# Half of the output gate's projection moves into the row-by-row stage of q, k and v, and group sums continue in PSUM

## The chip, the cores and the metric

The kernel runs on one core of a Trainium2 chip. The metric is the device time of one execution in microseconds; of several runs the median is taken. The engines are PE (matrix products), DVE (VectorE), ACT (ScalarE), POOL (GpSimd) and SP, whose queue issues the transfers here. PSUM is the memory in which PE adds up its products; SBUF is the memory that all engines share.

## The reference

The reference is a trunk of two layers in float32, with 256 rows (`S`) and 2048 columns (`DM`). Layer 0 has an mLSTM mixer and a squared-ReLU MLP, layer 1 a gated recurrence and an MLP. Each of the four sublayers norms its input and modulates it by a scale, a shift and a gate that are products of `silu(c)` with a 2048 x 6144 matrix (`ada`). What matters here is the mixer of layer 0:

```
def mlstm_mixer(h, w_in, b_gate, norm_g, w_out):
    proj = h @ w_in
    q, k, v, o, ig, fg = jnp.split(proj, [1024, 2048, 4096, 6144, 6152], axis=-1)   # 8 heads
    ...
    hh = mlstm_chunkwise(q, k, v, li, lf)          # two chunks of 128 rows, state carried over
    hh = hh * lax.rsqrt(jnp.mean(hh * hh, axis=-1, keepdims=True) + EPS)
    hh = hh.reshape(B, S, V_W) * norm_g
    return (hh * jax.nn.sigmoid(o)) @ w_out
```

(The split points are written out as numbers, and the reshaping is left out.) `o`, the output gate, is a product of `h` with 2048 columns of `w_in`; it is needed only where the heads are done. `ig` and `fg` feed the recurrence of the stabilised weights (`li`, `lf`).

## The kernel before

The product of every weight matrix runs over tiles of 128 x 2048 floats (1 MB). A tile comes by one transfer into a buffer (`raw`, four buffers, in `weights()`, L146), ACT rounds each half of it to a shorter format (`whi`, L153), and DVE forms the rest (`wlo`, L154). Activations are split in the same way (`pair`, L163 and L164). Three products, `whi` with both parts of the pair and `wlo` with the upper one, then replace one full product (`mm3`, L172 to L174). A tile may also go to PE unsplit, as one full float32 product (`direct`, the tile `wdir`): PE takes longer for it, ACT and DVE do nothing.

The modulation vectors are 192 more tiles of 1 MB (`adaraw`), which share the four buffers. Each is multiplied and summed by one DVE instruction (L113). They are needed step by step through the whole program and are spread over it as filler: `fill()` after a tile of weights issues the next adas at a rate, and `need()` issues those that the next step cannot do without. The rate comes from `QKV_RATE` in the first stage and later from `PACE`, which says how many adas are to be done at the end of each stage (56 at the end of stage `o`, 66 in `out0`).

The SP queue issues the transfers in the order of the program's lines. On the other engines a scheduler fixes the order of the instructions beforehand, by its own model of costs; the weights' split and the adas have a raised priority there. At run time every engine works its list from front to back, and an instruction that waits holds up all behind it.

The stages that the change touches:

- **Groups.** The normed input `h` comes as 16 chunks of 128 columns, and each needs its own two adas first. So q, k and v are computed by rows of the weight matrix: `GROUPS` = (2, 4, 4, 4, 2) chunks at a time (`group()`), each group with all 4096 columns of q, k, v. A group of n chunks takes 2n tiles (4, 8, 8, 8, 4; 32 in all); eight of these are direct (`DIRECT`, tile numbers). A group's sum for some columns is formed in PSUM, and `put()` takes it over: in the first group ACT copies it to SBUF (L390), in the later ones DVE adds it to what lies there (L392; 128x256 for q and k, 128x512 for v).
- **The gate block and its rows.** After the fourth group comes the block `wg` (L178 and L179) with the columns of `ig` and `fg`, then row arithmetic on eight partitions in DVE, then `rows` goes to DRAM (`rows_d`) and one column of it comes back to all partitions (`mlast`). From that and from the transposes of `g` (`gp`, L513, copied to `gT`) comes `wk` (L517, L518). The last group's products stand behind the gate block and are interleaved with this by the scheduler.
- **The heads.** Eight heads follow, each in parts: `scores`, `state` (`kw` and `cp`, L535 and L553), `head`, `meansq`, and after each second head `normed`, `gated`, which multiplies with the gate and forms the pairs `zs`. Between these parts stand the output gate's 16 blocks (`wo`, `ogate()`); the table `OB` says how many come at each of the 17 places. Each block ends in a tanh on ACT.
- **The output product.** 16 blocks of `awo` on the 16 z pairs, with the residual (L303) and the next norm; then the MLP.

Of the kernel before, what the change touches and what calls it, by code (L numbers as in the profile page):

```python
# [8 lines left out]
F32 = mybir.dt.float32  # L9
# [6 lines left out]
P = 128  # L16
# [24 lines left out]
GROUPS = (2, 4, 4, 4, 2)  # L41
DIRECT = (0, 1, 2, 3, 5, 8, 11, 14)

OB = (1, 1, 1, 1, 0, 1, 1, 1, 0, 1, 1, 1, 0, 1, 1, 1, 0)

QKV_RATE = (2, 1, 1, 0.75, 0)
PACE = dict(o=56, out0=66, w1a=82, w1b=90, mlp0=160, mix1=174, out1=176, mlp1=192)
# [3 lines left out]
def trunk_kernel(ctx, tc, xT_d, par_d, ada_d, wqkv_d, wg_d, wo_d, awo_d, bwi_d, bg_d, bwo_d,  # L51
# [335 lines left out]

    def put(dst, src, first):
        if first:
            A.activation(dst, src, AF.Copy)  # L390
        else:
            V.tensor_tensor(out=dst, in0=src, in1=dst, op=ALU.add)  # L392

# [8 lines left out]
    def group(gi, h32):  # L402
        gn, k0, nt = GROUPS[gi], sum(GROUPS[:gi]), 2 * sum(GROUPS[:gi])
        width = DM // gn
        for nb in range(2 * gn):
            direct = nt in DIRECT
            gh = h32 if direct else [[p[:, 0, :], p[:, 1, :]] for p in hs[k0:k0 + gn]]
            if direct:
                w = wpool.tile([P, DM], F32, name="wdir", tag="raw")
                nc.sync.dma_start(out=w, in_=wqkv_d[nt])  # L410
            else:
                w = weights(wqkv_d[nt])
            nt += 1

            def part(kk, o, n):
                if direct:
                    return [w[:, kk * width + o:kk * width + o + n]]
                o += kk % (gn // 2) * width
                return [t[:, o:o + n] for t in w[kk * 2 // gn]]

            def product(out, pairs, kk):
                ops = [(l, m) for a, l in enumerate(pairs[0]) for b, m in enumerate(pairs[1]) if a + b < 2]
                for n, (l, m) in enumerate(ops):
                    PE.matmul(out, lhsT=l, rhs=m, start=kk + n == 0,  # L424
                              stop=kk == gn - 1 and n == len(ops) - 1)

            for c0 in range(0, width, min(width, 512)):
                col = nb * width + c0
                if col < 2 * H * DQK:
                    for jj in range(min(width, 512) // P):  # L430
                        acc = ps.tile([P, S], F32, name="mm")
                        for kk in range(gn):
                            product(acc, (part(kk, c0 + jj * P, P), gh[kk]), kk)
                        n = col // P + jj
                        put(qk[n // 2][:, n % 2, :], acc, gi == 0)
                else:
                    n = min(width, 512)
                    for t in range(2):
                        acc = ps.tile([P, n], F32, name="mm")
                        for kk in range(gn):  # L440
                            product(acc, ([a[:, t * P:(t + 1) * P] for a in gh[kk]],
                                          part(kk, c0, n)), kk)
                        dst = vs[(col - 2048) // 512 * 2 + t].rearrange("p a b -> p (a b)")
                        o = (col - 2048) % 512
                        put(dst[:, o:o + n], acc, gi == 0)
            fill(1, QKV_RATE[gi])
# [8 lines left out]
    with ExitStack() as mctx:  # L455
# [130 lines left out]

        ths, hbs, zs = [], [], []
        obs = [0]

        def ogate(n):  # L590

            for _ in range(n):
                j = obs[0]
                obs[0] += 1
                acc = block([wo_d[j]], hs, mm3)
                if j % 2 == 0:
# [20 lines left out]

        pace("o", 16)
        ogate(OB[0])
# [220 lines left out]
```

## Time and profile before

| | |
|---|---|
| median of 3 runs | 2254.61 us (2252.55 to 2256.29) |
| profiled execution, its own time | 2257.06 us |
| its span | 2255.4 us |
| mean granted clock of PE | 0.991 |
| PE, DVE, ACT busy | 97%, 77%, 53% of the span |
| first matmul of group 1 | 61.51 us |
| end of the gate block | 214.1 us |
| `wk` | 254.53 us |
| last z pair | 380.1 us |
| end of the output product | 471.6 us |

All stages that the change touches lie in the first 472 us. Positions are counted from the start of the span. Busy time of PE is modelled: a matmul's record includes the drain of its pipeline, so records overlap. DVE's records, too, are a little longer than the spacing at which the same instructions follow each other. Windows of the profile give, for a stretch of time, the busy time of each engine with the number of its instructions, the clock granted to PE (1 is full speed), the busy share of the transfer engines, and what they moved in GB/s. In the chain of waits each row is a start, a duration and the work that held up the end; in groups of instructions, a row ends with the idle time just before the group's instructions and what ended it.

### The profile page before, as it was taken

What the parts mean: (1) busy time and instruction counts of PE and PEld (TensorE: products, weight loads), DVE (VectorE), ACT (ScalarE), POOL (GpSimd) and SP (SyncE); (2) the same over time, 40 slices, a digit from 0 to 9 for tenths busy, and PEclk for the clock granted to TensorE, in tenths of its full rate; (3) what the DMA queues carried; (4) which work ended last, traced back from release to release, by engine and by line L of the source; (5) the groups of instructions that cost most, each with busy time, mean ns of one, the idle gap of its engine ahead of it and who ended that gap; (6) DMA issues with size and microseconds to landing.
All of it is one profiled execution on the core that took longest, in us unless ns stands there. A gap on an engine that the chain in (4) does not pass through costs nothing.

```text
span 2255.4 us, 33736 instructions
## 1 busy us (share of the span) xinstructions
PE 2190.8 (97%) x13402; PEld 1942.1 (86%) x13402; DVE 1740.0 (77%) x2290; ACT 1194.7 (53%) x1845; POOL 79.4 (4%) x70
## 2 busy tenths in 40 slices
PE   7999999999999999999999999999999999999997
PEld 5788899898888888888888889888888888888886
DVE  5899899888998778888889898879775555555554
ACT  4334575454763336664445677756664334665443
POOL 0000000200000000000010000110000000000110
PEclk9999999999999999999999999999999999999999
DMA  9997788889788889888897677657776555555552
GB/s 341 340 345 286 276 308 327 322 291 329 272 303 317 317 317 329 324 322 320 310 323 251 225 241 267 222 205 260 281 280 205 187 187 188 188 189 191 188 188 101
DMA packets 85598, 601.24 MB, mean 267 GB/s; under 512 B 10424, under 2 KB 10552, under 8 KB 13120
## 3 DMA queue, kind: packets, MB, share of 16 engines
q1 hardware_dynamic: 84864, 598.03, 73.9%
q8 instruction: 105, 1.72, 0.3%
q10 hardware_dynamic: 576, 1.05, 0.1%
q14 instruction: 53, 0.43, 0.1%
HBM read 596.93 MB, written 2.11 MB: 266 GB/s over the span
## 4 chain that ended last, share of the span: by engine, by line
PE 81%; DVE 8%; DMA 5%; ACT 3%; issue 3%; POOLq 0%; DVEq 0%; SPq 0%; ACTq 0%
PE mm L178 40%; PE mm L179 21%; PE mm L424 6%; PE mm L174 3%; DVE wlo L154 3%; PE mm L173 3%; PE mm L172 3%; DMA adaraw<-in_ada 3%; DVE adaraw L113 2%; ACT whi L153 1%; PE mm L196 1%; PE mm L195 1%; PE mm L197 1%; DVE hmod L278 0%; DVE pair L167 0%
## 5 line engine op out<-in xcount | busy, mean ns | idle before, releaser
L178 PE MATMUL mm<-pair,whi 128*128 128x512 f32 x4352 | 1528.9, 395 | 7.1 <-DVE pair L167 5.5
L179 PE MATMUL mm<-pair,wlo 128*128 128x256 f32 x4352 | 1218.9, 281 | 9.2 <-DVE wlo L154 9.1
L154 DVE TENSOR_TENSOR wlo<-raw,whi 128x1024 fp32r<-128x1024 f32 x722 | 876.9, 1223 | 355.7 <-ACT whi L153 354.3
L153 ACT ACTIVATE whi<-raw 128x1024 fp32r<-128x1024 f32 x722 | 760.3, 1058 | 707.4 <-PE mm L178 503.1
L178 PEld LDWEIGHTS mm<-pair,whi 128*128 128x128 f32 x4352 | 817.1, 188 | 199.3 <-DVE pair L167 4.5
L179 PEld LDWEIGHTS mm<-pair,wlo 128*128 128x128 f32 x4352 | 819.1, 188 | 15.6 <-DVE wlo L154 13.6
L113 DVE SCALAR_TENSOR_TENSOR adaraw<-adaraw,cbc 128x2050 f32<-128x2050 f32 x192 | 439.6, 2290 | 74.4 <-DMA adaraw<-in_ada 63.4
L174 PE MATMUL mm<-pair,wlo 128*128 128x256 f32 x880 | 250.4, 285 | 3.0 <-DVE wlo L154 3.0
L172 PE MATMUL mm<-pair,whi 128*128 128x256 f32 x880 | 250.9, 285 | 2.4 <-ACT whi L153 2.4
L173 PE MATMUL mm<-pair,whi 128*128 128x256 f32 x880 | 250.6, 285 | 0.0
L174 PEld LDWEIGHTS mm<-pair,wlo 128*128 128x128 f32 x880 | 168.9, 192 | 3.7 <-DVE wlo L154 3.6
L172 PEld LDWEIGHTS mm<-pair,whi 128*128 128x128 f32 x880 | 168.7, 192 | 3.4 <-ACT whi L153 2.6
L173 PEld LDWEIGHTS mm<-pair,whi 128*128 128x128 f32 x880 | 168.9, 192 | 0.1
L303 DVE SCALAR_TENSOR_TENSOR xall<-mm,mod,xall 128x256 f32<-128x256 f32 x171 | 82.1, 481 | 36.5 <-PE mm L179 25.7
L312 ACT ACTIVATE hsum<-hsum 128x256 f32<-128x256 f32 x124 | 50.6, 414 | 107.9 <-DVE hsum L229 95.9
L258 POOL TENSOR_TENSOR nacc<-nacc,nsq 128x256 f32<-128x256 f32 x52 | 64.1, 1233 | 379.9 <-ACT nsq L249 369.8
L424 PE MATMUL mm<-pair,whi 128*128 128x256 f32 x384 | 69.5, 287 | 4.7 <-ACT whi L153 3.7
L424 PEld LDWEIGHTS mm<-pair,whi 128*128 128x128 f32 x384 | 59.0, 192 | 6.7 <-ACT whi L153 5.0
L424 PE MATMUL mm<-whi,pair 128*128 128x512 f32 x192 | 62.0, 399 | 0.6 <-DVE qk L392 0.6
L256 POOL TENSOR_TENSOR nacc<-nsq 128x256 f32<-128x256 f32 x4 | 6.3, 1568 | 1451.2 <-ACT nsq L249 1451.2
L164 DVE TENSOR_TENSOR pair<-hsum,pair 128x256 fp32r<-128x256 f32 x128 | 52.8, 419 | 1.9 <-ACT pair L163 1.5
L163 ACT ACTIVATE pair<-hsum 128x256 fp32r<-128x256 f32 x128 | 52.5, 415 | 3.2
(197 smaller groups left out, 1521.6 us busy)
## 6 DMA issues: line engine op xcount, KB each, us to landing
raw<-in_w SPq DMA_DIRECT2D x220, 1024.0 KB, 5.2
adaraw<-in_ada SPq DMA_DIRECT2D x192, 1025.0 KB, 7.0
raw<-in_w1a SPq DMA_DIRECT2D x32, 1024.0 KB, 7.0
raw<-in_bwi SPq DMA_DIRECT2D x28, 1024.0 KB, 5.1
raw<-in_wqkv SPq DMA_DIRECT2D x24, 1024.0 KB, 7.1
raw<-in_wo SPq DMA_DIRECT2D x16, 1024.0 KB, 7.0
raw<-in_awo SPq DMA_DIRECT2D x16, 1024.0 KB, 7.2
raw<-in_bwo SPq DMA_DIRECT2D x16, 1024.0 KB, 4.9
```

The costliest lines, as they stand in the source:

```text
L113: V.scalar_tensor_tensor(out=raw, in0=raw, scalar=1.0, in1=cbc, op0=ALU.mult, op1=ALU.mult, accum_out=mod[i][:, j:j + 1])
L153: A.activation(hi, sl, AF.Copy)
L154: V.tensor_tensor(out=lo, in0=sl, in1=hi.bitcast(F32), op=ALU.subtract)
L164: V.tensor_tensor(out=lo, in0=src, in1=hi.bitcast(F32), op=ALU.subtract)
L172: PE.matmul(out, lhsT=whi, rhs=p[:, 0, :], start=first, stop=False)
L173: PE.matmul(out, lhsT=whi, rhs=p[:, 1, :], start=False, stop=False)
L174: PE.matmul(out, lhsT=wlo, rhs=p[:, 0, :], start=False, stop=last)
L178: PE.matmul(out, lhsT=whi, rhs=p.rearrange("p a t -> p (a t)"), start=first, stop=False)
L179: PE.matmul(out[:, 0:S], lhsT=wlo, rhs=p[:, 0, :], start=False, stop=last)
L258: G.tensor_tensor(out=self.acc, in0=self.acc, in1=sq, op=ALU.add)
L303: V.scalar_tensor_tensor(out=xT[j], in0=acc[:, a:a + S], scalar=mod[i][:, 32 + j:33 + j], in1=xT[j], op0=ALU.mult, op1=ALU.add)
L424: PE.matmul(out, lhsT=l, rhs=m, start=kk + n == 0, stop=kk == gn - 1 and n == len(ops) - 1)
```

## The change

The first stage now also computes 1024 of the output gate's 2048 columns (`OG` = 8 blocks of 128). A group of n chunks takes 2.5 n tiles (5, 10, 10, 10, 5; 40 in all), and the number of tiles per group is `per`. Direct are now the five tiles of group 0 alone; the other 35 are split. The eight `wo` blocks left stand one to a head, after `state`. The four SBUF tiles of the moved half (`ob`) get their tanh in place, 128x512 each.

`put()` is gone. A sum is now 128x512 throughout: two column blocks of 256 side by side for q, k and the gate, 512 columns for v. From group 1 on, ACT first copies the sum so far from SBUF into PSUM, PE goes on adding to it (`start` is false for all its products), and ACT copies the result back. That makes 80 copies into PSUM and 100 out of it; the 96 additions on DVE are gone.

The rates `QKV_RATE` become (1.6, 0.8, 0.8, 0.4, 0) per tile, so 8, 8, 8 and 4 adas are issued with groups 0 to 3 (before 8, 8, 8 and 6); with four that group 0 needs in advance 32 adas lie before the heads, before 34. `PACE` is as it was: 56 are done after the heads. So 24 adas (before 22) are spread over 8 blocks of `wo` (before 16).

```diff
-DIRECT = (0, 1, 2, 3, 5, 8, 11, 14)
+DIRECT = (0, 1, 2, 3, 4)
+OG = 8
-OB = (1, 1, 1, 1, 0, 1, 1, 1, 0, 1, 1, 1, 0, 1, 1, 1, 0)
+OB = (0, 1, 0, 1, 0, 1, 0, 1, 0, 1, 0, 1, 0, 1, 0, 1, 0)
-QKV_RATE = (2, 1, 1, 0.75, 0)
+QKV_RATE = (1.6, 0.8, 0.8, 0.4, 0)
...
-    def put(dst, src, first):
-        if first:
-            A.activation(dst, src, AF.Copy)
-        else:
-            V.tensor_tensor(out=dst, in0=src, in1=dst, op=ALU.add)
+    ob = [act.tile([P, 2, S], F32, name="th", tag="act") for s in range(OG // 2)]
...
-        gn, k0, nt = GROUPS[gi], sum(GROUPS[:gi]), 2 * sum(GROUPS[:gi])
+        gn, k0 = GROUPS[gi], sum(GROUPS[:gi])
+        per = (4096 + OG * P) // 512
+        nt = per * k0 // 4
         width = DM // gn
-        for nb in range(2 * gn):
+        for nb in range(per * gn // 4):
...
-                    PE.matmul(out, lhsT=l, rhs=m, start=kk + n == 0,
-                              stop=kk == gn - 1 and n == len(ops) - 1)
+                    PE.matmul(out, lhsT=l, rhs=m, start=clear and kk + n == 0,
+                              stop=kk == gn - 1 and n == len(ops) - 1, skip_group_check=True)
...
+                for t in range(2):
+                    acc = ps.tile([P, 512], F32, name="mm")
+                    if col < 2048:
+                        dst = qk[col // 256 + t]
+                    elif col < 4096:
+                        dst = vs[(col - 2048) // 512 * 2 + t]
+                    else:
+                        dst = ob[(col - 4096) // 256 + t]
+                    dst = dst.rearrange("p a b -> p (a b)")
+                    if gi > 0:
+                        A.activation(acc, dst, AF.Copy)
+                    if 2048 <= col < 4096:
                         for kk in range(gn):
                             product(acc, ([a[:, t * P:(t + 1) * P] for a in gh[kk]],
-                                          part(kk, c0, n)), kk)
+                                          part(kk, c0, 512)), kk, gi == 0)
+                    else:
+                        for jj in range(2):
+                            for kk in range(gn):
+                                product(acc[:, jj * S:(jj + 1) * S],
+                                        (part(kk, c0 + (2 * t + jj) * P, P), gh[kk]), kk,
+                                        gi == 0 and jj == 0)
+                    A.activation(dst, acc, AF.Copy)
             fill(1, QKV_RATE[gi])
...
-        obs = [0]
+        obs = [OG]
+        ths = list(ob)
+        for th in ths:
+            A.activation(th, th, AF.Tanh, scale=0.5)
...
-        pace("o", 16)
+        pace("o", 16 - OG)
```

The line numbers of the new file are some six to ten higher from the groups on, and one higher before.

Three places show how the order of the engines' lists moves. The first is SP's list in the stage of the heads, where `in_wo` is a block of the output gate, `in_ada` an ada, and `MB` the rows that a head needs. Before:

```order
70 L526 DMA MB<-rows_d 128x512
71 L146 DMA raw<-in_wo 128x2048
72 L111 DMA adaraw<-in_ada 128x2050
73 L526 DMA MB<-rows_d 128x512
74 L146 DMA raw<-in_wo 128x2048
75 L111 DMA adaraw<-in_ada 128x2050 x2
76 L146 DMA raw<-in_wo 128x2048
77 L111 DMA adaraw<-in_ada 128x2050
78 L526 DMA MB<-rows_d 128x512
```

After:

```order
63 L532 DMA MB<-rows_d 128x512
64 L147 DMA raw<-in_wo 128x2048
65 L112 DMA adaraw<-in_ada 128x2050 x3
66 L532 DMA MB<-rows_d 128x512
67 L147 DMA raw<-in_wo 128x2048
68 L112 DMA adaraw<-in_ada 128x2050 x3
69 L532 DMA MB<-rows_d 128x512
```

A head had about two blocks and three adas between its `MB` and the next; it now has one block and three adas.

The second is DVE's list around `wk` and the first heads (`E`, `qw`, `em` and `rs` belong to a head). Before:

```order
208 L113 SCALAR_TENSOR_TENSOR adaraw,mod_127<-adaraw,cbc 128x2050
209 L154 TENSOR_TENSOR wlo<-raw,whi 128x1024 x2
210 L517 TENSOR_TENSOR wk<-gT,mlast 128x8
211 L113 SCALAR_TENSOR_TENSOR adaraw,mod_127<-adaraw,cbc 128x2050
212 L542 SCALAR_TENSOR_TENSOR E<-sp,E 128x256
213 L545 SCALAR_TENSOR_TENSOR qw<-qk_187,qw 128x128
214 L113 SCALAR_TENSOR_TENSOR adaraw,mod_127<-adaraw,cbc 128x2050
```

After:

```order
123 L114 SCALAR_TENSOR_TENSOR adaraw,mod_127<-adaraw,cbc 128x2050
124 L155 TENSOR_TENSOR wlo<-raw,whi 128x1024
125 L523 TENSOR_TENSOR wk<-gT,mlast 128x8
126 L155 TENSOR_TENSOR wlo<-raw,whi 128x1024
127 L114 SCALAR_TENSOR_TENSOR adaraw,mod_127<-adaraw,cbc 128x2050 x2
128 L155 TENSOR_TENSOR wlo<-raw,whi 128x1024
129 L551 SCALAR_TENSOR_TENSOR qw<-qk_187,qw 128x128
130 L548 SCALAR_TENSOR_TENSOR E<-sp,E 128x256
131 L155 TENSOR_TENSOR wlo<-raw,whi 128x1024 x2
132 L551 SCALAR_TENSOR_TENSOR qw<-qk_187,qw 128x128
133 L114 SCALAR_TENSOR_TENSOR adaraw,mod_127<-adaraw,cbc 128x2050
```

The weight halves of the last group now stand on both sides of `wk`, and two adas follow it ahead of the first head's own work.

On PE, `gp` (the transposes of `g`, which `rows` and `wk` follow) moves at the same place. Before, it stood ahead of the last three of group 4's 144 products (96 of 256 columns, 48 of 512):

```order
575 L424 MATMUL mm<-whi,pair 128x512 x2
576 L424 MATMUL mm<-wlo,pair 128x512
577 L424 MATMUL mm<-whi,pair 128x512
578 L513 MATMUL gp<-ident,g 128x8 x2
579 L424 MATMUL mm<-whi,pair 128x512
580 L424 MATMUL mm<-wlo,pair 128x512
```

After, it stands behind 96 narrow and 20 wide products of 192 (144 narrow, 48 wide):

```order
844 L425 MATMUL mm<-whi,pair 128x512 x2
845 L425 MATMUL mm<-wlo,pair 128x512
846 L519 MATMUL gp<-ident,g 128x8
847 L425 MATMUL mm<-whi,pair 128x512
848 L519 MATMUL gp<-ident,g 128x8
849 L425 MATMUL mm<-whi,pair 128x512
850 L425 MATMUL mm<-wlo,pair 128x512
```

The rest of group 4's v and all of its gate columns follow `gp`.

The third is ACT's list at the same place, in the kernel after (L440 is the copy into PSUM, L451 the copy out of it, L597 the tanh of the moved half):

```order
269 L440 ACTIVATE mm<-th 128x512
270 L154 ACTIVATE whi<-raw 128x1024 x2
271 L451 ACTIVATE v_202<-mm 128x512
272 L524 ACTIVATE wk<-wk 128x8
273 L440 ACTIVATE mm<-th 128x512 x2
274 L451 ACTIVATE th<-mm 128x512
275 L541 ACTIVATE kw<-kp,wk 128x128
276 L451 ACTIVATE th<-mm 128x512
277 L597 ACTIVATE th<-th 128x512 x2
```

ACT's part of `wk` stands ahead of the last two copies into PSUM; before, no product of the groups waited for ACT beyond the weights' upper halves.

More of the change, by code (lines that the diff above doesn't have):

```diff
@@ L419, in part, with product @@
                 return [t[:, o:o + n] for t in w[kk * 2 // gn]]
-            def product(out, pairs, kk):
+            def product(out, pairs, kk, clear):
                 ops = [(l, m) for a, l in enumerate(pairs[0]) for b, m in enumerate(pairs[1]) if a + b < 2]
                 for n, (l, m) in enumerate(ops):
-                    PE.matmul(out, lhsT=l, rhs=m, start=kk + n == 0,
-                              stop=kk == gn - 1 and n == len(ops) - 1)
-            for c0 in range(0, width, min(width, 512)):
+                    PE.matmul(out, lhsT=l, rhs=m, start=clear and kk + n == 0,
+                              stop=kk == gn - 1 and n == len(ops) - 1, skip_group_check=True)
@@ L428, in group @@
+            for c0 in range(0, width, 512):
                 col = nb * width + c0
[L429 to L439, printed above, removed]
+                for t in range(2):
[10 more added lines that the diff above has]
+                    if 2048 <= col < 4096:
@@ L440, in group @@
                         for kk in range(gn):
                             product(acc, ([a[:, t * P:(t + 1) * P] for a in gh[kk]],
-                                          part(kk, c0, n)), kk)
-                        dst = vs[(col - 2048) // 512 * 2 + t].rearrange("p a b -> p (a b)")
-                        o = (col - 2048) % 512
-                        put(dst[:, o:o + n], acc, gi == 0)
+                                          part(kk, c0, 512)), kk, gi == 0)
[5 more added lines that the diff above has]
+                                        gi == 0 and jj == 0)
@@ L585, in meansq @@
             V.scalar_tensor_tensor(out=out, in0=ss, scalar=1.0 / DV, in1=em, op0=ALU.mult, op1=ALU.add)
-        ths, hbs, zs = [], [], []
-        obs = [0]
+        hbs, zs = [], []
+        obs = [OG]
+        ths = list(ob)
+        for th in ths:
+            A.activation(th, th, AF.Tanh, scale=0.5)
         def ogate(n):
@@ L594, in ogate @@
                 obs[0] += 1
-                acc = block([wo_d[j]], hs, mm3)
+                acc = block([wo_d[j - OG]], hs, mm3)
                 if j % 2 == 0:
@@ L803 @@
     for gn in GROUPS:
-        w = w_in[k0 * P:(k0 + gn) * P, 0:4096].reshape(gn, P, 2 * gn, DM // gn)
-        qkv.append(w.transpose(2, 1, 0, 3).reshape(2 * gn, P, DM))
+        cs = 4096 + OG * P
+        w = w_in[k0 * P:(k0 + gn) * P, 0:cs].reshape(gn, P, cs * gn // DM, DM // gn)
+        qkv.append(w.transpose(2, 1, 0, 3).reshape(cs * gn // DM, P, DM))
         k0 += gn
@@ L814 @@
         "wg": cols(wg)[0],
-        "wo": cols(w_in[:, 4096:6144]),
+        "wo": cols(w_in[:, 4096 + OG * P:6144]),
         "awo": cols(a["a_w_out"][0]),
```

## The prediction

> **What bounds the kernel now.** I read the stages first (busy time of each engine in stretches that I cut at group 1's first matmul, at the ends of the groups, at `wk`, at the last z pair and at the split of the ninth `awo` tile), then the chain of waits inside them, then the groups of instructions by line.
>
> ```profile
> core 0: us, PE busy (x) PEld busy (x) DVE busy (x) ACT busy (x) POOL busy (x), PEclk, DMA share, GB/s
> 0.00:61.50 61.50, 44.11 (x160) 31.19 (x160) 33.08 (x45) 26.96 (x59) 0.70 (x6) 0.94 0.90 340
> 61.50:112.20 50.70, 50.68 (x257) 39.73 (x257) 43.76 (x60) 15.15 (x22) 0.00 (x0) 0.97 0.90 340
> 112.20:163.40 51.20, 49.02 (x282) 41.81 (x280) 48.03 (x64) 18.71 (x24) 0.00 (x0) 1.00 0.94 353
> 163.40:214.10 50.70, 49.88 (x314) 44.98 (x315) 47.89 (x60) 20.16 (x23) 0.00 (x0) 1.00 0.87 321
> 214.10:254.50 40.40, 36.48 (x249) 32.36 (x248) 35.28 (x64) 15.98 (x19) 0.00 (x0) 1.00 0.52 176
> 254.50:380.10 125.60, 124.38 (x985) 120.99 (x986) 118.95 (x167) 83.68 (x158) 8.28 (x8) 0.99 0.89 327
> 380.10:426.10 46.00, 40.60 (x313) 39.99 (x312) 43.02 (x69) 20.33 (x35) 10.61 (x6) 0.93 0.89 318
> 426.10:471.70 45.60, 45.60 (x388) 45.57 (x387) 36.76 (x38) 21.52 (x27) 10.48 (x8) 1.00 0.90 322
> ```
>
> Up to 61.5 transfers set the pace (340 GB/s, PE idle for 17.4 of 61.5 us). In the rows of groups 1 to 3 (61.5 to 214.1) PE is busy for all but 3.0 us, with DVE close behind (48 of 51); ACT has more than half free. In 254.5 to 380.1, the heads with the output gate's blocks between them, PE and DVE are both nearly full: 124.4 and 119.0 of 125.6. From 426 on PE alone is the bound. So the program has one stage in which neither PE nor DVE has room, and the change takes PE work out of that stage but leaves most of its DVE work.
>
> ```profile
> L113 DVE SCALAR_TENSOR_TENSOR adaraw<-adaraw,cbc 128x2050 f32<-128x2050 f32 x22 | 50.2, 2284 | 0.0
> L113 DVE DVE_READ_ACCUMULATOR adaraw<-adaraw,cbc 128x1 f32 x22 | 1.8, 80 | 0.0
> L154 DVE TENSOR_TENSOR wlo<-raw,whi 128x1024 fp32r<-128x1024 f32 x30 | 36.1, 1223 | 0.7 <-ACT whi L153 0.7
> L113 DVE SCALAR_TENSOR_TENSOR adaraw<-adaraw,cbc 128x2050 f32<-128x2050 f32 x7 | 16.0, 2285 | 0.0
> L154 DVE TENSOR_TENSOR wlo<-raw,whi 128x1024 fp32r<-128x1024 f32 x14 | 17.2, 1258 | 1.0 <-ACT whi L153 1.0
> ```
>
> The first three rows are DVE's groups of 254.5 to 380.1, the last two those of 380.1 to 426.1. Adas and weight halves are 88 of its 119 us in the first of these stages; the other 30.9 are the attention's own.
>
> **Group 0 (start of group 1).** The change puts 5 whole tiles ahead of group 1 where there were 4, with the same 8 adas (1.6 times 5, before 2 times 4). A tile of 1.05 MB at 340 GB/s takes 3.1 us, so group 1 starts 3 to 5 us later; I take 65.5 in place of 61.5. The fifth tile's products (some 6.8 us) lie in PE's idle time there.
>
> **Groups 1 to 3 and the gate block.** Split tiles replace four direct ones, and six more tiles come in.
>
> ```profile
> 69.01 7.07 PE L424 MATMUL mm<-hdirect,wdir 128*128 128x256 f32 x32
> 213.80 0.28 PE L179 MATMUL mm<-pair,wlo 128*128 128x256 f32 x1
> 61.51 1.27 PE L424 MATMUL mm<-pair,whi 128*128 128x256 f32 x5 [3.72 <-ACT whi L153]
> 61.50:65.10 3.60, 3.59 (x16) 3.31 (x17) 3.08 (x5) 2.03 (x4) 0.00 (x0) 0.53 0.96 392
> ```
>
> The stretch 163.4 to 214.1 holds eight split tiles and the gate block (its last matmul is the second row): 50.7/9 = 5.63 us for a tile. A direct one is the first row, about 6.8 us without the drain of its last matmul. Before, groups 1 to 3 and the gate block are 20 x 5.63 + 4 x 6.8 + 5.63 = 145 us and took 152.6, so 7 us were lost: about 2 at the start, where the clock was 0.53 for 3.6 us after 3.72 us of idle PE (last two rows), the rest to late halves on DVE. After: 31 x 5.63 = 174.5. Of the losses I keep 4, since DVE's additions go:
>
> ```profile
> L392 DVE TENSOR_TENSOR qk<-mm,qk 128x256 f32<-128x256 f32 x48 | 18.7, 418 | 2.9 <-PE mm L424 2.5
> L392 DVE TENSOR_TENSOR v<-mm,v 128x512 f32<-128x512 f32 x24 | 16.0, 684 | 2.4 <-PE mm L424 2.3
> L153 ACT ACTIVATE whi<-raw 128x1024 fp32r<-128x1024 f32 x44 | 45.4, 1056 | 51.5 <-PE mm L424 28.1 <-DMA raw<-in_wqkv 17.1 <-PE mm L178 3.4
> L390 ACT ACTIVATE v<-mm 128x512 f32<-128x512 f32 x8 | 4.8, 597 | 11.0 <-PE mm L424 11.0
> ```
>
> These additions are 34.7 us of DVE in 152.6, standing between its weight halves. In their place ACT copies each sum into PSUM and out again. Out of PSUM a 128x512 copy took 0.597 us (last row). Into PSUM none is in the trace: below by the 128x256 addition's 0.418, above by the 128x1024 copy's 1.056 us; nearest in shape and engine is the 0.597 row, which I take. (The Trainium skill, "ScalarE: Activation LUTs", says that ScalarE writes PSUM faster than SBUF; no row of this trace shows a write to PSUM of this size. By it the copy would be under 0.6.) ACT then has for a tile of four chunks 2 x 1.06 + 4 x 0.60 + 0.3 (its share of `hdirect` and pairs) = 4.8 us against PE's 5.63: covered, and in the order the copies in stand one or two units ahead of PE. Transfers: 10 tiles and 8 adas at 3.1 us are 55.8 against 56.3 of PE, so the cover is thin and half of the 4 us kept is for that. The gate block then ends at 65.5 + 178.5 = 244, before at 214.1.
>
> **From the gate block to wk.** Here the path is rows arithmetic, two small transfers, and `wk`.
>
> ```profile
> 239.20 0.29 PE L513 MATMUL gp<-ident,g 8*128 8x8 f32 x2
> 242.28 4.66 DMA rows_d<-rows
> 246.95 7.55 DMA mlast<-rows_d
> 254.53 0.18 DVE wk L517
> L517 DVE TENSOR_TENSOR wk<-gT,mlast 128x8 f32<-128x8 f32 x1 | 0.2, 169 | 2.9 <-DMA mlast<-rows_d 2.9
> ```
>
> Before it takes 40.4 us: 25 to `gp` (behind all but three of group 4's products on PE), 3 to the rows' transfer, 12.2 to `wk`. After, the order puts `gp` behind 116 of 192 products of group 4, 96 narrow and 20 wide: 2 tiles and 20/24 of one, 16 us at 5.63. But group 4 (two chunks) does four units per tile, so ACT needs 2.1 + 8 x 0.6 = 6.9 us where PE needs 5.6; I take 17 (16 to 20). DVE's side, some 10 us of rows arithmetic and four halves, fits in that. So `wk` comes at 244 + 17 + 3 + 12.2 = 276, 21.7 us later than the 254.5 of before, while eight of sixteen `wo` blocks, 45 us of PE, are already done. The wait for `mlast` now has more behind it: ACT's `wk` stands ahead of the last copies into PSUM, so PE's last units of group 4 wait too.
>
> **The heads.** From `wk` on DVE is the longer of the two. By the order it runs, from `wk` to the split of the ninth `awo` tile, 30 adas and 36 halves; before it was 29 and 44 (the five rows above). That is the core of it: eight blocks less take away eight halves in this stretch (the others' halves lay before `wk` or are replaced by the `awo` tiles' own), and the adas, three per block now, are as many as ever.
>
> ```profile
> 132.87 2.22 DVE adaraw L113 x2
> 222.19 2.28 DVE wlo L154 x2
> 164.22 44.23 PE mm L424 x280
> ```
>
> At the spacing of the chain (2.22 for an ada with its accumulator, 1.14 for a half) and with 30.9 + 9.2 us of other work (busy time of the two stages without these groups), DVE's work in this stretch was 29 x 2.22 + 44 x 1.14 + 40.1 = 154.6 of the 171.6 us that it took, with 17.0 of gaps; now it is 30 x 2.22 + 36 x 1.14 + 40.1 = 147.7. PE per head needs 5.63 + 4.6 = 10.2 us (4.6 from 124.4 less 15.5 tiles, over eight heads), DVE 3 x 2.22 + 2 x 1.14 + 3.9 = 12.8, transfers four tiles and 0.25 MB, 13.0. So PE idles some 2.7 us in each head, transfers are level with DVE, and the gaps that DVE had from a full PE shrink while some from transfers come. I take gaps of 10, with 0 and 17 as ends.
>
> **Sum.** The ninth `awo` tile is split at 276 + 147.7 + 10 = 434 in place of 426.1: 7.6 us later. From there on PE is the bound and the program is the same (56 adas at the end of the heads, then the same pace), so nothing is won back. The four tanh of 128x512 replace eight of 256 and cost ACT nothing that shows. The profiled execution took 2257.06 us (span 2255.4) and would become 2264.7; it lies 2.4 above the median of 2254.61, to which I add the 7.6: **2262 us**.
>
> The Trainium skill ("Perfetto Trace Analysis", Optimization Strategy) says that where the most contended engine changes between regimes, interleaving the regimes may help. By it this change goes the wrong way for the heads: it takes PE's work out from between DVE's. The stage rows agree as far as they go.
>
> **Rivals.** *A, PE is the bound throughout and DVE's relief is a gain.* For it: PE is busy for 97% of the whole span,
>
> ```profile
> PE 2190.8 (97%) x13402; PEld 1942.1 (86%) x13402; DVE 1740.0 (77%) x2290; ACT 1194.7 (53%) x1845; POOL 79.4 (4%) x70
> ```
>
> and DVE loses 34.7 us of additions in groups 1 to 3 alone. Then the idle PE of the six stages 61.5 to 426.1 goes (0.0 + 2.2 + 0.8 + 3.9 + 1.2 + 5.4 = 13.5), four direct tiles become split (4 x 1.2 = 4.7), and group 0 does 6.8 us of work in 4: together 21, 2234 us; with half of it, 2244. Against it: adas and attention's DVE work stay after `wk`. The Trainium skill ("Perfetto Trace Analysis", Optimizing Scalar/DVE Operations) has the rule that work moves to ScalarE where DVE is saturated; DVE's rows agree before 214 only. *B, a wash.* If ACT doesn't hold group 4 (16 in place of 17), groups 1 to 3 lose 2 less, and gaps are 7, the sum is 276 - 3 + 147.7 + 7 - 426.1 = 1.6: 2256 us. *C, ACT becomes the bound, and the time is longer still.* If the copy into PSUM costs 1.06, a four-chunk tile needs 2.1 + 1.2 + 2.1 + 0.3 = 5.7 (level with PE) and one of group 4 2.1 + 2.4 + 4.2 = 8.7 against 5.6: 2.8 tiles to `gp` cost 9 us more than PE's own, 8 more than I allow; with the 7.6, 2270. It decides from 0.75 us for that copy on. The same 2269 comes if the gaps stay at 17. *D, PE's clock.* Idle of 2.7 us in each head may bring what the 0.53 row shows, at 1.7 us a time; PE's slack of 2.7 covers it, so I give it nothing of its own.
>
> **How the numbers follow.** About 0.2%, 4.5 us, is what a measurement of this kernel can tell from no change. The forecast (4.5 to 12 us more) has 0.36, C and equal gaps (over 12) 0.15, B (within 4.5) 0.27, A in whole or part 0.22. Faster 0.22, same 0.27, slower 0.51. The likeliest case alone is 2259 to 2267; the range reaches down to half of A and up past C: 2243 to 2274.
>
> **What would show it.** Right: group 1's first matmul at 64 to 67; gate block's end at 241 to 247; `wk` at 272 to 281; between `wk` and the last z pair DVE busy for over 90% and PE for under 85%; the ninth `awo` tile's split 3 to 12 us later than before; the rest shifted as a whole. The additions' place in groups 1 to 3 shows ACT at 75 to 85%. Wrong: PE busy for over 95% in the heads (A); ACT busy for over 95% in groups 1 to 4 (C); the later part of the program not shifted but shorter or longer by itself, or `wk` before 268.

## The result, and the profile after

The changed kernel took 2276.19 us (median of 4 runs, 2271.14 to 2277.94) beside 2253.58 us for the kernel before on the same chip: a ratio of 1.0096 with a 95% interval of 1.0069 to 1.0123. It is slower by 1.0%, some 22 us. The forecast was slower by 7.6 us, and the measured time lies above the range. The profiled executions are 2275.65 us (span 2273.9) and 2257.06 us (span 2255.4).

The stages of the changed kernel, cut at the same events as those of before (the second to fourth rows are groups 1 to 3 with the gate block, then gate block to `wk`, `wk` to the last z pair, from there to the split of the ninth `awo` tile, and on to the end of the output product):

```profile
core 0: us, PE busy (x) PEld busy (x) DVE busy (x) ACT busy (x) POOL busy (x), PEclk, DMA share, GB/s
0.00:68.10 68.10, 51.22 (x192) 37.69 (x192) 33.03 (x43) 29.63 (x58) 0.70 (x6) 0.92 0.88 334
68.10:130.00 61.90, 60.81 (x382) 55.37 (x383) 47.35 (x48) 46.90 (x72) 0.00 (x0) 0.94 0.87 312
130.00:190.00 60.00, 59.84 (x403) 54.34 (x401) 46.59 (x45) 48.04 (x71) 0.00 (x0) 1.00 0.92 327
190.00:252.30 62.30, 62.20 (x407) 56.06 (x406) 36.95 (x35) 45.62 (x67) 0.00 (x0) 1.00 0.73 260
252.30:281.60 29.30, 26.00 (x165) 22.44 (x164) 21.40 (x37) 27.91 (x45) 0.00 (x0) 1.00 0.49 151
281.60:408.40 126.80, 106.89 (x773) 101.03 (x772) 117.17 (x170) 76.59 (x151) 8.05 (x8) 0.93 0.84 319
408.40:448.00 39.60, 35.96 (x278) 35.34 (x277) 37.49 (x60) 18.56 (x33) 9.49 (x6) 0.93 0.85 319
448.00:493.20 45.20, 45.20 (x385) 45.20 (x384) 37.17 (x38) 21.55 (x27) 10.19 (x8) 1.00 0.92 329
```

The row of the heads says most. With seven blocks of the gate less in it than before, the stage takes 126.8 us; it took 125.6. In exchange 37 products of group 4 and some more of `awo` lie in it, so PE's busy time fell by 17.5 us. PE stands idle for 19.9 us, before for 1.2. PE's work went out of the stage and no time came out with it, while the work was added to the groups, where PE has no room. DVE has 117.2 us of work in 126.8:

```profile
L114 DVE SCALAR_TENSOR_TENSOR adaraw<-adaraw,cbc 128x2050 f32<-128x2050 f32 x25 | 57.0, 2285 | 0.6 <-DMA adaraw<-in_ada 0.6
L155 DVE TENSOR_TENSOR wlo<-raw,whi 128x1024 fp32r<-128x1024 f32 x22 | 26.2, 1219 | 4.5 <-ACT whi L154 4.5
L579 DVE SCALAR_TENSOR_TENSOR em<-em,ad 128x256 f32<-128x256 f32 x8 | 3.4, 420 | 2.5 <-ACT ad L578 2.5
L591 DVE SCALAR_TENSOR_TENSOR rs<-hss,em 128x256 f32<-128x256 f32 x8 | 3.3, 418 | 1.6 <-PE hss L590 1.6
```

These are DVE's groups in the heads; its idle time is spread over waits for upper halves and for the attention's own steps. What the wait looks like on PE, in the timeline between two heads and in the clock behind it:

```profile
341.06 0.33 PE L539 MATMUL kp<-ident,qk 128*128 128x128 f32 x1
345.69 0.48 PE L173 MATMUL mm<-pair,whi 128*128 128x256 f32 x1 [4.30 <-ACT whi L154]
341.00:345.50 4.50, 0.36 (x2) 0.14 (x1) 4.50 (x9) 4.06 (x9) 0.52 (x1) 1.00 1.00 375
345.50:349.00 3.50, 2.73 (x11) 2.44 (x12) 3.50 (x7) 1.64 (x4) 0.00 (x0) 0.55 0.59 237
```

PE waits 4.3 us for the next block's upper half while DVE is full (4.50 of 4.50) and transfers are too (1.00); then its clock is at 0.55. The upper half is ACT's work, and ACT is busy for 4.06 of the 4.50 us with parts of the heads that stand ahead of it in its list, so the row alone doesn't say which of the engines is late.

ACT's groups in groups 1 to 3 give the price of the copies:

```profile
L154 ACT ACTIVATE whi<-raw 128x1024 fp32r<-128x1024 f32 x64 | 66.3, 1051 | 6.3 <-PE mm L425 5.1 <-PE mm L179 0.8
L440 ACT ACTIVATE mm<-v 128x512 f32<-128x512 f32 x24 | 14.4, 600 | 0.6
L451 ACT ACTIVATE v<-mm 128x512 f32<-128x512 f32 x24 | 14.3, 595 | 7.7 <-PE mm L425 7.6
```

A copy into PSUM (L440) took 0.600 us and one out of it 0.595: the row that the forecast took, 0.597, was right for both. The Trainium skill ("ScalarE: Activation LUTs", Step-by-step: what each stage is for) has writes to PSUM faster than to SBUF. These two rows don't test it, since the source changes with the destination; the nearest row with both sides in SBUF, the tanh of 128x512 (L597), took 0.641 us (median of four), which agrees as far as another function can show it.

### The profile page after: what moved, and what is told of

It is laid out like the page before. It is cut to its first block, busy times and chain, and to the rows that moved or that the text cites. A ratio compares the mean times of both kernels' runs of the same rounds, so it can differ in the third digit from the quotient of the medians.

```text
span 2273.9 us, 33867 instructions
## 1 busy us (share of the span) xinstructions
PE 2195.6 (97%) x13434; PEld 1950.5 (86%) x13434; DVE 1709.5 (75%) x2200; ACT 1284.3 (56%) x2003; POOL 78.1 (3%) x70
## 4 chain that ended last, share of the span: by engine, by line
PE 78%; DVE 9%; DMA 6%; issue 4%; ACT 3%; DVEq 0%; POOLq 0%; POOL 0%; SPq 0%; ACTq 0%
PE mm L179 38%; PE mm L180 19%; PE mm L425 8%; DMA adaraw<-in_ada 3%; DVE wlo L155 3%; PE mm L175 3%; PE mm L173 3%; PE mm L174 3%; DVE adaraw L114 3%; ACT whi L154 1%; PE mm L197 1%; DMA raw<-in_w1a 1%; PE mm L196 1%; PE mm L198 1%; DMA raw<-in_bwi 1%
## 5 line engine op out<-in xcount | busy, mean ns | idle before, releaser
L180 PE MATMUL mm<-pair,wlo 128*128 128x256 f32 x4352 | 1217.0, 280 | 9.1 <-DVE wlo L155 9.1
L180 PEld LDWEIGHTS mm<-pair,wlo 128*128 128x128 f32 x4352 | 819.6, 188 | 16.0 <-DVE wlo L155 13.8
L173 PE MATMUL mm<-pair,whi 128*128 128x256 f32 x752 | 217.0, 289 | 14.2 <-ACT whi L154 13.8
L175 PE MATMUL mm<-pair,wlo 128*128 128x256 f32 x752 | 217.5, 289 | 9.1 <-DVE wlo L155 9.0
L174 PE MATMUL mm<-pair,whi 128*128 128x256 f32 x752 | 215.5, 287 | 0.0
L175 PEld LDWEIGHTS mm<-pair,wlo 128*128 128x128 f32 x752 | 146.6, 195 | 11.5 <-DVE wlo L155 11.5
L425 PE MATMUL mm<-pair,whi 128*128 128x256 f32 x672 | 123.0, 286 | 5.7 <-ACT whi L154 5.5
L425 PE MATMUL mm<-pair,wlo 128*128 128x256 f32 x336 | 94.7, 291 | 2.8 <-DVE wlo L155 2.7
L425 PE MATMUL mm<-whi,pair 128*128 128x512 f32 x224 | 70.7, 395 | 0.0
L425 PEld LDWEIGHTS mm<-pair,wlo 128*128 128x128 f32 x336 | 63.5, 192 | 5.5 <-DVE wlo L155 5.1
```

What stands on the lines that cost most here:

```text
L173: PE.matmul(out, lhsT=whi, rhs=p[:, 0, :], start=first, stop=False)
L174: PE.matmul(out, lhsT=whi, rhs=p[:, 1, :], start=False, stop=False)
L175: PE.matmul(out, lhsT=wlo, rhs=p[:, 0, :], start=False, stop=last)
L180: PE.matmul(out[:, 0:S], lhsT=wlo, rhs=p[:, 0, :], start=False, stop=last)
L425: PE.matmul(out, lhsT=l, rhs=m, start=clear and kk + n == 0, stop=kk == gn - 1 and n == len(ops) - 1, skip_group_check=True)
```

## The experiments

Times are compared as ratios to the kernel before on the same chip, since its median differs by a few microseconds from chip to chip. Positions and spans of stages come from the profiled execution of each.

### More adas before the heads

```diff
-QKV_RATE = (1.6, 0.8, 0.8, 0.4, 0)
+QKV_RATE = (1.6, 0.8, 0.8, 0.8, 0.8)
```

> The changed kernel with 8 adas more before the heads: rate 0.8 in groups 3 and 4 (there 0.4 and 0), so 40 adas are done before the heads and 16 instead of 24 lie in them. Theory (DVE's adas bound the heads, transfers have room in groups 3 and 4): the heads (wk to last z pair) go from 126.8 to about 110 us, groups 3 and 4 grow by at most 3, the time falls by 12 to 17 us against the changed kernel, to about 2260. Rival (transfers bound the heads): the heads shrink too, by 8 x 3.1 = 25 us of transfers at most, but groups 3 and 4, which take those transfers, show late weight tiles. Rival (the cost is in the copies of sums in the groups): the time stays within 4 us of the changed kernel.

Measured: 2261.47 us, ratio 1.0052 (1.0035 to 1.0070), so about 10 us below the changed kernel (12 to 17 were expected) and still slower than before. Gate block to `wk`, and the heads:

```profile
250.10:294.80 44.70, 39.15 (x253) 35.09 (x251) 36.81 (x51) 35.99 (x58) 0.00 (x0) 0.92 0.72 246
294.80:393.80 99.00, 90.56 (x688) 86.18 (x689) 92.06 (x149) 69.73 (x138) 8.85 (x8) 0.97 0.84 317
```

The heads became 27.8 us shorter, where 17 were expected, but the stage ahead of them 15.4 us longer, where at most 3 were. The adas of group 4 push its weight tiles and `mlast` back, and part of the heads' PE work was done behind `wk` before and lies ahead of it now (88 products more in the first row than in the changed kernel, 85 fewer in the second). Over both stages together 12.4 us are saved. Adas in the heads cost, but which of their two loads does, transfer or DVE, this run can't tell.

### Adas with one load each

The next three runs leave the program's order as it is (the scheduler may place neighbours differently) and take away the load of the heads' 24 adas: DVE's part, the transfer's, and both. First DVE's (2 columns instead of 2050):

```diff
+        n = 2 if 32 < len(done) <= 56 else ADA
         with tc.high_priority(offset=APRIO):
-            V.scalar_tensor_tensor(out=raw, in0=raw, scalar=1.0, in1=cbc, ...
+            V.scalar_tensor_tensor(out=raw[:, 0:n], in0=raw[:, 0:n], scalar=1.0, in1=cbc[:, 0:n], ...
```

> The changed kernel, but the 24 adas of the heads are multiplied in two of their 2050 columns only, so these modulation vectors are not computed; the tiles are transferred whole. It prices DVE's part against the transfers'. Theory (DVE bounds the heads): the heads fall from 126.8 us to what PE needs, 85 to 95 us, or to the transfers' 13.0 a head, 104 us, whichever is longer. Rival (transfers bound them already): they stay at 120 us or more.

Then the transfer's, with DVE at full length on a constant tile (and a short operation on the 64 columns that come, so that the transfer is still waited for):

```diff
+        short = 32 < len(done) <= 56
+        if short:
+            nc.sync.dma_start(out=raw[:, 0:64], in_=ada_d[i, j][:, 0:64])
+        else:
             nc.sync.dma_start(out=raw, in_=ada_d[i, j])
...
-            V.scalar_tensor_tensor(out=raw, in0=raw, scalar=1.0, in1=cbc, ...
+            V.scalar_tensor_tensor(out=raw, in0=cbc if short else raw, scalar=1.0, in1=cbc, ...
```

> The counterpart of the run with short multiplications: the 24 adas of the heads bring 64 of their 2050 columns only (32 KB in place of 1 MB), while DVE still multiplies at full length, on data that is in SBUF already (so these modulation vectors are not computed). Theory 1 (DVE alone bounds the heads): wk to the last z pair stays at 120 to 127 us. Theory 2 (transfers alone): it falls to DVE's own 12.8 a head, 103 to 110. Theory 3 (neither alone: the wait goes round from DVE to the four shared buffers, to the next transfer, and back): it falls by some 5 to 15 us as the short multiplications did, from 126.4 to 112 to 121.

And both:

```diff
+        n = 64 if 32 < len(done) <= 56 else ADA
-        nc.sync.dma_start(out=raw, in_=ada_d[i, j])
+        nc.sync.dma_start(out=raw[:, 0:n], in_=ada_d[i, j][:, 0:n])
...
+            V.scalar_tensor_tensor(out=raw[:, 0:n], in0=raw[:, 0:n], scalar=1.0, in1=cbc[:, 0:n], ...
```

> Both at once: the 24 adas of the heads bring and multiply 64 columns only, so neither DVE nor the transfers have their load of adas in the heads. What is left is one block of the gate and the attention per head. Theory (adas bound the heads, in whichever way): wk to the last z pair falls to PE's 10.2 us a head with small losses, 82 to 95 us. Rival (the order and the latencies between PE, ACT and DVE in each head bound them): it stays above 105.

Measured: 2267.81 us (ratio 1.0077, 1.0053 to 1.0102) without DVE's load, 2274.22 us (1.0105, 1.0073 to 1.0136) without the transfers, 2248.80 us (0.9983, 0.9963 to 1.0002) without both. The heads of the three, in this order, each from its `wk` to its last z pair:

```profile
279.00:399.30 120.30, 105.26 (x771) 99.18 (x770) 69.77 (x166) 75.96 (x151) 4.49 (x8) 0.95 0.87 334
```

```profile
281.40:408.00 126.60, 107.31 (x784) 101.79 (x785) 118.34 (x191) 77.14 (x153) 7.26 (x8) 0.92 0.44 151
```

```profile
281.00:384.00 103.00, 97.95 (x763) 94.04 (x762) 72.23 (x167) 75.15 (x149) 5.27 (x8) 0.99 0.52 175
```

Without the transfers DVE is as full as ever (118.3 of 126.6) and the stage as long. (The 22 short operations of this run are 4.3 us more for DVE, so up to about that much relief may be hidden in it.) Without DVE's load, 47 us of DVE's busy time are gone (117.2 to 69.8) and the stage is only 6 us shorter, with transfers at 334 GB/s; taking the transfers away as well makes it 17 us shorter still. Without both it falls by 24 us in all, and PE is busy for 98 of 103: it is the bound then. So in the changed kernel DVE and the transfers each hold the heads by themselves, at about the same length, and relieving one of them shows little. The rival of order and latencies (above 105) falls with the last run, in which PE is nearly dense, though 103.0 is only just below its line. The theory's 82 to 95 was missed too: it counted one block and the attention per head, while the stage also holds work on `awo` and the last products of group 4. The first of the three by itself met its rival's condition (120 us or more: transfers bind); the second shows that this was half of the answer.

The four shared buffers tie the two together. SP's waits in the heads of the changed kernel:

```profile
SPq L112 <- DVE adaraw L114: 50.7, 17, 7.9
SPq L147 <- DVE adaraw L114: 8.0, 3, 4.4
```

and in the heads of the kernel before:

```profile
SPq L111 <- DVE adaraw L113: 30.5, 8, 5.4
SPq L146 <- DVE adaraw L113: 21.5, 8, 4.6
```

(The columns are microseconds, times, longest.) SP holds the next transfer until DVE has done with the tile in its buffer: 59 us of the stage behind adas alone, and 52 us before. So the wait isn't new, and since the run without transfers was no shorter, this queue isn't what makes DVE late. Whether it is why transfers are at 0.84 (before at 0.89) and not at more was not tested.

### The same in the kernel before

If PE's blocks had been a cover for the adas, they must have cost nothing where sixteen blocks lay between them. The edit is that of the last run, made in the kernel before, where 22 adas lie in the heads (`34 < len(done) <= 56`).

> The kernel before with the 22 adas of its heads shortened in transfer and multiplication to 64 columns (so these modulation vectors are not computed), as was done with the 24 of the changed kernel, where the heads fell by 24 us (126.4 to 102.5) and the time by about 26. Theory (in the kernel before, sixteen blocks of PE work cover the adas, so they cost nothing there): wk to the last z pair stays at 120 to 125.6 us and the time falls by 0 to 9 us, most of it after the heads. Rival (adas cost the same in any order): the heads fall by 15 us or more, the time by 20 or more.

Measured: 2244.18 us beside 2251.63, ratio 0.9962 (0.9929 to 0.9995), within what the theory gave. The heads:

```profile
250.90:375.10 124.20, 121.25 (x979) 118.43 (x979) 82.85 (x176) 83.29 (x157) 3.93 (x8) 1.00 0.55 184
```

They took 124.2 us, before 125.6: 22 adas cost the heads 1.4 us there, and 24 adas cost them 24 us in the changed kernel. In the whole time, by the ratios, leaving this load out is worth about 8.6 us in the kernel before (1 to 0.9962) and 25 in the changed one (1.0096 to 0.9983), so the adas account for some 17 of the 22 us. With the load gone from both, the changed kernel is about 5 us slower, which is no more than the intervals of the two ratios allow for no difference.

### The sums alone, and the move alone

One run keeps all columns where they were and only changes the way of the sums:

```diff
-DIRECT = (0, 1, 2, 3, 4)
-OG = 8
+DIRECT = (0, 1, 2, 3, 5, 8, 11, 14)
+OG = 0
-QKV_RATE = (1.6, 0.8, 0.8, 0.4, 0)
+QKV_RATE = (2, 1, 1, 0.75, 0)
```

(`OB`, too, is that of before.)

> Only the sums: none of the gate's columns move (OG = 0, the direct tiles, the table OB and the rates of before), but sums go on in PSUM from what ACT wrote there. Theory (the loss is in the heads, the sums' new way is a gain): groups 1 to 3 lose less of PE than before (152.6 us there), group 4 and the way to wk shorten by some us, heads as before; 3 to 8 us faster than before. Rival (the copies of sums cost): slower than before by some us.

The other moves the columns and leaves the sums to DVE:

```diff
-                    if gi > 0:
-                        A.activation(acc, dst, AF.Copy)
...
-                    A.activation(dst, acc, AF.Copy)
+                    if gi == 0:
+                        A.activation(dst, acc, AF.Copy)
+                    else:
+                        V.tensor_tensor(out=dst, in0=acc, in1=dst, op=ALU.add)
```

(and each group's products clear their sum).

> Only the move: half of the gate's columns in the groups as in the changed kernel, but sums of later groups are added by DVE in 128x512 pieces as before. Theory: DVE gets 80 additions of 0.68 us = 55 us more in groups 1 to 4, where it had 8 to 14 us free per group of 60; groups 1 to 3 grow by 5 to 15 us, heads stay at 126 to 128; 5 to 20 us slower than the changed kernel. Rival (the copies of sums cost more than additions): as fast as the changed kernel or faster.

Measured: the sums alone 2251.43 us, ratio 1.0010 (0.9996 to 1.0023), no difference from before, where 3 to 8 us of gain were expected. The move alone 2278.97 us, ratio 1.0127 (1.0102 to 1.0151), about 7 us above the changed kernel, though the intervals overlap. Groups 1 to 3 with the gate block, and gate block to `wk`, for the sums alone and then for the move alone:

```profile
62.00:217.60 155.60, 152.29 (x850) 127.48 (x851) 111.21 (x111) 105.87 (x164) 0.00 (x0) 0.98 0.90 331
217.60:255.00 37.40, 32.97 (x209) 28.70 (x209) 27.99 (x41) 29.69 (x48) 0.00 (x0) 0.95 0.56 193
```

```profile
68.30:252.90 184.60, 180.74 (x1186) 163.65 (x1187) 164.04 (x186) 74.41 (x87) 0.00 (x0) 0.99 0.83 299
252.90:291.20 38.30, 36.57 (x247) 32.46 (x245) 34.67 (x59) 15.52 (x20) 0.00 (x0) 1.00 0.48 154
```

Groups 1 to 3 do not get shorter: 155.6 us with sums in PSUM and 152.6 without, 184.2 in the changed kernel and 184.6 with additions. DVE's busy time fell by 28 us there (139.7 worked out from the three rows of before, 111.2 now), and no time came out with it. The way from the gate block to `wk` is shorter with the sums in PSUM: by 3.0 us without the move (40.4 to 37.4) and by 9 us with it (38.3 to 29.3). The 9 us come with another order of PE's list: `gp` stands behind 171 of PE's products of this stage in the run of the move alone and behind 114 in the changed kernel, and comes 29.2 and 19.5 us after the gate block. So they are the scheduler's placing of `gp` in the main, and not the price of an addition against a copy; and 3.0 is little more than one profile differs from another (1.9 in a run below that keeps the additions). The expectation that additions would lengthen groups 1 to 3 by 5 to 15 us failed; the loss of the move alone is the heads' again.

### Other rates

Two adas fewer before the heads than in the first run of this section:

```diff
-QKV_RATE = (1.6, 0.8, 0.8, 0.4, 0)
+QKV_RATE = (1.6, 0.8, 0.8, 0.8, 0.4)
```

> The changed kernel with rates 0.8 and 0.4 in groups 3 and 4: 38 adas before the heads (changed kernel 32, the run with 0.8 and 0.8 had 40). In that run wk came 13 us later than in the changed kernel, behind the adas of group 4, and the heads were 27 us shorter. Theory (the adas of group 3 are free, those of group 4 cost their transfers ahead of its weights): wk at 283 to 289, heads 100 to 108, the time 2 to 6 us below that run. Rival (every ada costs the same wherever it lies): 3 to 5 us above that run.

Measured: 2263.61 us, ratio 1.0061 (1.0030 to 1.0091).

```profile
248.70:284.90 36.20, 31.72 (x200) 28.20 (x199) 29.05 (x44) 32.59 (x53) 0.00 (x0) 0.95 0.63 210
284.90:395.30 110.40, 99.14 (x746) 94.16 (x745) 99.84 (x152) 72.86 (x144) 10.66 (x8) 0.97 0.83 307
```

`wk` at 284.9 was as expected, the heads at 110.4 are 2 us longer than that, and the time doesn't differ clearly from the run with 40. With 32, 38 and 40 adas ahead, the stretch from the gate block to the last z pair is 156.1, 146.6 and 143.7 us: 1.6 us for each of the first six, 1.5 for the last two. The rival, the same price for every ada, fits this stretch better than the theory.

Three runs looked for a kernel faster than both, with the sums in PSUM and no move, or as before:

```diff
-QKV_RATE = (2, 1, 1, 0.75, 0)
+QKV_RATE = (2, 1, 1, 1, 0.5)
-PACE = dict(o=56,
+PACE = dict(o=60,
```

> None of the gate's columns move and sums go on in PSUM, as in the run with OG = 0, but 4 adas more come before the heads (rates 1 and 0.5 in groups 3 and 4, before 0.75 and 0) and 60 instead of 56 are done after the heads. Theory: transfers are idle for half of the stage from the gate block to wk (0.52 busy), so these adas cost nothing there; the heads keep their 22 adas, the output product has 4 fewer (DVE was late there, PE lost 5.4 us in 380 to 426): 3 to 6 us faster than the kernel before. Rival (the adas delay the last group's weights and mlast): wk is later by as much, no gain.

(the kernel with the sums alone). And in the kernel before, `(2, 1, 1, 1, 0)` or `(2, 1, 1, 0.75, 0.5)`, both with `o=58`:

> The kernel before, with the one lever that shortened the changed kernel: 2 adas more in group 3 (rate 1 for 0.75; transfers there are 0.87 busy), 58 for 56 after the heads, so the heads keep 22 and the output product has 8 for 10. Theory: group 3 has room for 2 transfers (6.6 us idle of 50.7), DVE there is at 47.9 of 50.7 and loses 1 to 3; the output product, where PE lost 7.5 us at 400 to 420, wins 2 to 5: 0 to 4 us faster than before. Rival: DVE's lateness only moves from the output product to group 3, no difference.

> The same with the 2 adas in group 4 (rate 0.5 there for 0, group 3 as before), where transfers are 0.52 busy. Theory: their transfers and 4.4 us of DVE stand ahead of the rows' arithmetic and mlast, so wk comes 3 to 8 us later and eats the gain of the output product: within 3 us of before, or slower. Rival (free room there): 2 to 5 us faster.

Measured: 2256.09 us, ratio 1.0022 (1.0005 to 1.0039); 2255.09 us, 1.0001 (0.9988 to 1.0014); 2251.15 us, 0.9995 (0.9981 to 1.0009). In the first, groups 1 to 3 and the way to `wk` grew:

```profile
61.90:224.30 162.40, 154.73 (x850) 127.33 (x851) 115.01 (x115) 105.46 (x165) 0.00 (x0) 0.98 0.90 330
224.30:268.40 44.10, 41.15 (x269) 37.34 (x268) 36.52 (x51) 31.13 (x48) 0.00 (x0) 0.92 0.71 239
389.40:430.00 40.60, 40.60 (x346) 40.60 (x345) 37.68 (x61) 21.48 (x36) 8.01 (x6) 1.00 0.80 296
```

The output product ran without a gap on PE (40.60 of 40.60), as expected, and its gain was paid for ahead of `wk`: 6.8 us in groups 1 to 3 and 6.7 on the way to `wk` against the sums alone. The second, with two adas more in group 3, gave the same picture on a smaller scale:

```profile
61.70:220.10 158.40, 151.07 (x850) 126.17 (x851) 144.05 (x186) 53.88 (x68) 0.00 (x0) 0.99 0.92 339
```

5.8 us longer than the 152.6 of before. In the third the way to `wk` was not longer but 1.9 us shorter:

```profile
211.80:250.30 38.50, 33.54 (x200) 28.00 (x198) 33.81 (x63) 13.41 (x16) 0.00 (x0) 0.96 0.50 172
```

so its expected cost was wrong; yet the total is that of before. None of the runs beats the kernel before beyond its interval, apart from one that leaves work out (0.9929 to 0.9995, both loads short in the kernel before).

## Why the prediction was right and wrong

The direction, the place and the mechanism were right: from `wk` on DVE was the longer of the two, and PE idled in the heads (106.9 busy of 126.8, "under 85%"; DVE at 92%). The size was wrong: 7.6 us were forecast and 22.5 us stand at the ninth `awo` tile, which is split at 448.6 instead of 434. `wk` came 27.1 us later, and the stretch behind it was shorter by 4.6 us where 13.9 were forecast. Of the positions named as signs, group 1's start (68.1), the gate block's end (252.3) and the split lie outside, and `wk` (281.6) just outside. By the terms of the sum:

- **Group 0**, forecast 65.5: group 1 began at 68.1, 2.6 later than forecast. Counted from the first product (25.5 before, 25.9 after), the start came 6.1 us later, above the 3 to 5 that one tile of transfers gave. The step "the fifth tile's products (some 6.8 us) lie in PE's idle time there" failed:

```profile
25.50:61.50 36.00, 30.97 (x96) 19.74 (x96) 21.44 (x25) 15.12 (x34) 0.00 (x0) 0.92 0.89 331
25.90:68.10 42.20, 37.83 (x128) 25.99 (x128) 21.40 (x23) 17.88 (x33) 0.00 (x0) 0.93 0.87 328
```

  Of the 17.4 us that PE was idle before, only 5.0 lie behind the first product, and 3.7 of these are the wait just ahead of group 1. So the 6.9 us of the fifth tile's products lengthened the stretch; after, the wait ahead of group 1 is still there (4.0). In the chain of waits PE's products hold the shared buffers until group 1's first tile can be issued at 57.0, and it lands at 67.0.
- **Groups 1 to 3**, forecast 178.5: 184.2, 5.7 more. Some 1.6 us of it is the clock after group 0:

```profile
68.12 0.74 PE L425 MATMUL mm<-pair,whi 128*128 128x256 f32 x4 [4.03 <-ACT whi L154]
68.10:72.00 3.90, 3.11 (x13) 2.60 (x14) 3.88 (x5) 3.81 (x7) 0.00 (x0) 0.66 0.99 361
72.00:76.00 4.00, 4.00 (x21) 4.00 (x20) 3.41 (x5) 0.00 (x0) 0.00 (x0) 0.50 0.65 238
76.00:80.00 4.00, 4.00 (x32) 3.79 (x32) 0.80 (x1) 3.01 (x4) 0.00 (x0) 0.98 0.79 283
```

  By these rows the low clock cost 3.3 us (0.34 of 3.9 and 0.50 of 4.0), before 1.7 (0.47 of 3.6). The rest is small: PE's records cover 182.84 of the 184.2 us, and what spreads its products was not separated. The step "of the losses I keep 4, since DVE's additions go" failed: the run with additions is as long in this stage (184.6), so the additions had cost PE little or nothing there.
- **Gate block to `wk`**, forecast 32.2: 29.3. `gp` came at 19.5 us, not 17, but the two transfers behind it were quicker than the 12.2 taken from before:

```profile
271.76 0.22 PE L519 MATMUL gp<-ident,g 8*128 8x8 f32 x1
273.49 0.35 SPq L513 DMA_DIRECT2D rows_d<-rows  x1
275.63 0.38 SPq L515 DMA_DIRECT2D mlast<-rows_d  x1
281.59 0.17 DVE L523 TENSOR_TENSOR wk<-gT,mlast 128x8 f32<-128x8 f32 x1 [0.54 <-DMA mlast<-rows_d]
```

  From the rows' issue to `wk` it is 8.1 us. The term is 2.9 too long by two errors of opposite sign, so that it is no further off is luck.
- **Heads and output product**, forecast 147.7 of DVE's work and 10 of gaps: 167.0 from `wk` to the split, 9.3 more. This is the largest failed step. The stretch as one window, before and after:

```profile
254.50:426.10 171.60, 164.98 (x1295) 160.97 (x1296) 161.97 (x235) 104.01 (x192) 18.89 (x14) 0.97 0.89 324
281.60:448.60 167.00, 143.45 (x1054) 136.97 (x1053) 155.26 (x230) 95.15 (x184) 17.54 (x14) 0.93 0.84 319
```

  DVE was busy for 161.97 us before and 155.26 after, so it was idle for 9.6 us and then for 11.7. The forecast had 154.6 of work and 17.0 of gaps before. It took the other work as the stages' busy time less the full records of adas and halves, and then put adas and halves in at their shorter spacing; so the overlap of the records was taken off twice, and some 7.4 us of work went into the gaps. With the same 7.4 in its work (155.1), the forecast left DVE 2.6 us of idle time in the changed kernel, where 11.7 came. By the rows of the heads above and those of 408.4 to 448,

```profile
L155 DVE TENSOR_TENSOR wlo<-raw,whi 128x1024 fp32r<-128x1024 f32 x12 | 14.9, 1259 | 0.8 <-ACT whi L154 0.8
L114 DVE SCALAR_TENSOR_TENSOR adaraw<-adaraw,cbc 128x2050 f32<-128x2050 f32 x6 | 13.7, 2279 | 0.0
```

  the stretch holds 31 adas and 34 halves (30 and 36 were forecast, which makes nearly the same sum); so by the forecast's own measure the work was right (148 us), and the gaps were 17.0 before and 19 after. The step "the gaps that DVE had from a full PE shrink" failed: they didn't shrink, and before only 1.7 us of DVE's idle time had been ended by PE and 6.9 by ACT. After, ACT again ends most of it:

```profile
DVE wlo L155 <- ACT whi L154: 5.3, 7, 1.0
DVE em L579 <- ACT ad L578: 2.5, 4, 0.9
```

  Equal gaps stood in the forecast as the upper end, with too little weight. That transfers were level with DVE (13.0 and 12.8 a head) isn't what made the gaps: in the run without the transfers DVE is idle for 8.3 us of the heads, and for 9.6 in the changed kernel. Why ACT's parts come late to DVE was not tested and stays open.

The four deviations are 2.6 + 5.7 - 2.9 + 9.3 = 14.7, and with the 7.6 they make the 22.3.

Of the rivals, A (PE the bound throughout) is refuted: PE is busy for 84% of the heads, and DVE's relief in the groups gained nothing alone and nothing clear of noise in the changed kernel (7 us against the move alone, with intervals that overlap). B, a wash, fell with the time. C had two ways to 2269 and 2270. That of a dear copy into PSUM fell (0.600 us, and ACT at 76% in groups 1 to 3, where the forecast said 75 to 85); that of equal gaps is what came, on top of a later `wk`. D, the clock, showed itself (0.93 in the heads, 0.99 before), but whether it costs anything beyond the wait that brings it was not separated. That nothing is won back later is not refuted: in the two profiles the distance was 22.5 us at the ninth tile (448.6 to 426.1) and 18.5 at the end of the span, while the medians of the runs are 22.6 apart.

The Trainium skill's rule on regimes ("Perfetto Trace Analysis", Optimization Strategy), that interleaving stages with different bounds may help, was borne out in the reverse direction: taking PE's blocks from between DVE's adas made the adas cost 24 us in the heads, where they had cost 1.4.

## What to carry to other kernels

Work of one engine that is spread among another's is a cover; before it is moved, the time of the stage must be worked out as what remains without it, and here that was two loads, DVE's adas and their transfers, of the same length. To find out whether a stage is held by one thing or by two, take away each load alone and then both: here 6, 0 and 24 us, where either of the first two alone would have told a wrong story. And the gaps of a forecast must be counted by the same measure as its work, and kept as they were unless the trace names what ended them: here idle time put down to a full PE was for the most part ended by ACT, and it stayed.

## What the runs showed of the hardware that was not expected

A copy of 128x512 floats by ACT took as long into PSUM (0.600 us) as out of it (0.595). In the kernel before, PE's clock was at 0.53 for 3.6 us behind a wait of 3.72 us, with PE dense from then on (3.59 busy of 3.60). In the changed kernel, behind a wait of 4.03 us, it was at 0.66 for 3.9 us that held only 3.11 us of work, at 0.50 for 4.0 us more, and at 0.98 from 76.0 on. That the thinner work is the reason was not tested.
